# The decay and rate products of an RWKV-7 branch, taken in two passes of split operands; two staging buffers for raw weights

## The chip, the core and the metric

The kernel runs on one core of one Trainium2 chip. The metric is the time of one execution on the device, in microseconds (us); of a kernel that was run several times the median counts. One of the executions was recorded by the hardware profiler. Its page and its trace give the times of single instructions, of waits and of transfers. The engines go by the profile's names: PE is the matrix engine (PEld its weight loads), DVE the vector engine, ACT the scalar engine, POOL the GpSimd engine, and SP the engine whose queue issues all of this kernel's DMAs.

## What is computed

One layer over 2048 tokens of width 1024. The normalised input `h` is projected by one wide matrix into three branches and their gates: an RWKV-7 branch (8 heads of 64, with a delta-rule state), a sliding-window attention and a cross attention into 256 memory tokens. Each branch is gated and projected back, the three are merged by sigmoid gates, and a last projection is added to the input. All inputs and the output are float32.

The part that the change touches is the decay and the rate of the RWKV-7 branch, two products of low rank (64):

```
lw = token_shift_mix(p_w, mu_wa[0])
la = token_shift_mix(p_a, mu_wa[1])
w_log = -softplus(-(w0 + tanh(lw) @ w2)) - 0.5
decay = exp(-exp(w_log))
a = sigmoid(a0 + la @ a2)
```

`w2` and `a2` are 64 by 512. In the kernel they lie in one tile `w2a2`, `w2` in partitions 0 to 63 and `a2` in 64 to 127.

## The kernel before

**Blocks of tokens.** `build` runs four blocks of 512 tokens (the loop at L831). Tokens lie along the free axis, channels along the partitions. For each block: the low-rank inputs are projected and shifted (`proj` and `shift`, L832 and L833, then a tanh over the upper half of the partitions, L834); then two streams of work are woven together by given costs (`weave`, L865). `stream_r` holds the RWKV branch, four pairs of heads one after the other (`rwkv_pair`). `stream_f` holds everything else: in the first block the keys and values of the memory (`mem_kv`), then cross attention, window attention, merges and gates. After the streams come the merge of the RWKV branch, the norm of the next block's input (`x_norm`) and the output projection. What a function issues in between its `yield`s goes out in one piece. A scheduler then orders the instructions of each engine, which run strictly in that order.

**Products in three passes.** The big products split each float32 operand into a rounded part (type `F32R`) and the rest, and add three products (`gemm3`, L180 to L182): rounded by rounded, rounded weights by the rest of the activations, and the rest of the weights by rounded activations. A block of weights is 128 by 512 raw numbers and feeds 12 matmuls of 128x512, or 6 for the memory's values (L344 to L346).

**Weight staging.** `wblock` (L155) makes a block ready. In the first block of tokens it loads the raw weights into a tile `wraw` (L161, SP), ACT writes the rounded part into `whl` (L162), POOL subtracts to get the rest (L163), and the finished pair is stored to DRAM (`k`, L166, SP). The pool has three buffers for `wraw` and three for `whl`. The later blocks of tokens load the finished pair straight into `whl` (L158). The memory's weights are used once and not stored. On SP the store of a block stands directly ahead of the load that takes over the raw buffer of that block.

**The low-rank products.** In each pair, behind the projection of the keys (`proj` at L380 and `shift` at L381), there are two plain float32 matmuls with 64 rows each, L383 from the upper half of the partitions and L385 from the lower half. They write the PSUM tiles `pw` and `pa`, from a ring of two buffers (`rw_ps`). ACT takes a tanh of each (L387, L389). Then the rest of the previous pair is done (`rest`, L580 to L592). Its four transposes (L584) need a tile of the same ring, which comes free when L387 has read `pw`.

**Small rings.** `rt` is a ring of six work tiles of 128x512 (`tmp`), `ibc` one of two tiles of 1 KB per partition, used for the squares of the norms (L201) and by the triangular solve (L456 to L462, L476).

Of the kernel before, what the change touches and what calls it, by code (L numbers as in the profile page):

```python
# [9 lines left out]
F32 = mybir.dt.float32  # L10
F32R = mybir.dt.float32r
BF16 = mybir.dt.bfloat16
I32 = mybir.dt.int32
AF = mybir.ActivationFunctionType
ALU = mybir.AluOpType
# [4 lines left out]
TB = 512  # L20
NG = 12
NRT = 6
# [6 lines left out]
B_R, B_K, B_V, B_WA, B_ZA, B_Q, B_SK, B_SV, B_ZB, B_XQ, B_ZC, B_G = 0, 4, 8, 12, 13, 17, 21, 22, 23, 27, 31, 35  # L29
# [12 lines left out]
def build(tc, A, nsb=4):  # L42
    nc = tc.nc
    es = ExitStack()
    V, S, G, PE = nc.vector, nc.scalar, nc.gpsimd, nc.tensor

    def pool(name, bufs, **kw):
        return es.enter_context(tc.tile_pool(name=name, bufs=bufs, **kw))

    cp = pool("cp", 1)  # L50
    wp = pool("wp", 3)
    xp = pool("xp", 1)
    hp = pool("hp", 1)
    rp = pool("rp", 1)
# [12 lines left out]
    def rw_ps():  # L67
        return ps.tile([128, 512], F32, name="rw", bufs=2)
# [13 lines left out]
    def const(name, shape, src=None):  # L82
        t = cp.tile(shape, F32, name="c_" + name)
        nc.sync.dma_start(t, A[name] if src is None else src)
        return t
# [22 lines left out]
    w2a2 = const("w2a2", [128, 512])  # L108

    def pcol(name, i=0):  # L110
        o, w = PV[name]
        return pv[:, o + i:o + i + 1]
# [13 lines left out]
    def dcol(name, i=0):  # L126
        return dv[:, DV[name][0] + i:DV[name][0] + i + 1]
# [27 lines left out]
    def wblock(src, key=None):  # L155
        w = wp.tile([128, 2, 512], F32R, name="whl")
        if key in kept:
            nc.sync.dma_start(w.bitcast(F32), kept[key])  # L158
            return w[:, 0], w[:, 1]
        raw = wp.tile([128, 512], F32, name="wraw")  # L160
        nc.sync.dma_start(raw, src)  # L161
        S.activation(w[:, 0], raw, AF.Copy)  # L162
        G.tensor_tensor(w[:, 1], raw, w[:, 0].bitcast(F32), op=ALU.subtract)  # L163
        if key is not None and nsb > 1:
            kept[key] = dp.tile([128, 2, 512], F32, name=f"k{len(kept)}")
            nc.sync.dma_start(kept[key], w.bitcast(F32))  # L166
        return w[:, 0], w[:, 1]
# [50 lines left out]
    def proj(blk, hT, n=TB):  # L218
        o = mm_ps()
        gemm3(o[:, :n], [(w, (hT[0][:, k, :n], hT[1][:, k, :n])) for k, w in enumerate(wtiles(A["w_in"][blk], 8, ("in", blk)))])  # L220
        return o
# [142 lines left out]
    def shift(o, blk, mu, omu, sb, tag, bufs=1):  # L364
        t = rp.tile([128, TB], F32, name=tag, bufs=bufs)
        S.activation(t, o, AF.Copy, scale=omu)
        V.scalar_tensor_tensor(t[:, 1:], o[:, :TB - 1], mu, t[:, 1:], op0=ALU.mult, op1=ALU.add)
        V.scalar_tensor_tensor(t[:, 0:1], carry[sb % 2][:, blk:blk + 1], mu, t[:, 0:1], op0=ALU.mult, op1=ALU.add)
        V.tensor_copy(carry[1 - sb % 2][:, blk:blk + 1], o[:, TB - 1:TB])
        return t  # L370

    def tmp(tag="rt", bufs=NRT):
        return rp.tile([128, TB], F32, name=tag, bufs=bufs)

    EV, OD = slice(0, 64), slice(64, 128)
# [3 lines left out]
    def rwkv_pair(p, sb, hT, lwla, yas):  # L379
        kp = proj(B_K + p, hT)  # L380
        k = shift(kp, B_K + p, pcol("mu_k", p), dcol("omu_k", p), sb, "rk_")  # L381
        pw = rw_ps()
        PE.matmul(pw, w2a2[EV, p * 128:(p + 1) * 128], lwla[EV], start=True, stop=True)  # L383
        pa = rw_ps()
        PE.matmul(pa, w2a2[OD, p * 128:(p + 1) * 128], lwla[OD], start=True, stop=True)  # L385
        th = tmp()
        S.activation(th, pw, AF.Tanh, scale=0.5, bias=dcol("hw0", p))  # L387
        ta = tmp()
# [65 lines left out]
        for s in range(31):  # L454
            n = 31 - s
# [23 lines left out]
        for b in (0, 64):  # L479
            u, l = slice(b, b + 32), slice(b + 32, b + 64)  # L480
# [16 lines left out]
        for b in (0, 64):  # L497
            u, l = slice(b, b + 32), slice(b + 32, b + 64)
# [25 lines left out]
        for c in range(NC_):  # L524
            pw = rw_ps()[:, :C]
# [35 lines left out]
            for e, h, Q in HH:  # L561
                to = Sst[h, p] if c == NC_ - 1 else Z[h, e, c + 1]
# [222 lines left out]
    def merge(i, yh, yl, accs, hT, first=False, orange=range(8), gates=None):  # L785
        for o in orange:
            yield 3.718
            w = [t.rearrange("p (k c) -> p k c", k=4) for t in wblock(A["w_proj"][i, o], ("proj", i, o))]
            g = gates[o] if gates else gate(i, o, hT)
            pp = mm_ps()  # L790
            gemm3(pp, [((w[0][:, k], w[1][:, k]), (yh[k], yl[k])) for k in range(4)])
            if first:
                acc = mp.tile([128, TB], F32, name="mB")
                V.scalar_tensor_tensor(acc, g, 1.0, pp, op0=ALU.add, op1=ALU.mult)
                accs.append(acc)
            else:
                V.scalar_tensor_tensor(g, g, 1.0, pp, op0=ALU.add, op1=ALU.mult)  # L797
                V.tensor_tensor(accs[o], accs[o], g, op=ALU.add)
# [31 lines left out]
    hT = x_norm(0)  # L830
    for sb in range(nsb):  # L831
        wa = proj(B_WA, hT)  # L832
        lwla = shift(wa, B_WA, pcol("mu_wa"), dcol("omu_wa"), sb, "lwla")  # L833
        S.activation(lwla[EV], lwla[EV], AF.Tanh)  # L834
        yas = []
        ya, yb, yc_ = ([], []), ([], []), ([], [])
        accs = []

        def stream_r():
            for p in range(4):  # L840
                yield from rwkv_pair(p, sb, hT, lwla, yas)
            pend.pop()()
            yield 0.412

        def stream_f():
            if sb == 0:
                yield from mem_kv()
            for h in range(4):
                yield from cross_head(h, sb, hT, *yc_)
            rope_tables(sb)  # L850
            yield from swa_kv(sb, hT)
            yield 6.938
            for j in range(4):
                yield from weave(swa_pair(j, sb, hT, *yb), merge(2, *yc_, accs, hT, first=True, orange=(2 * j, 2 * j + 1)))
            yield from merge(1, *yb, accs, hT)
            for o in range(8):
                gates.append(gate(0, o, hT))
                yield 5.908

        gates = []  # L860
        def slower(g, f):
            for d in g:
                yield f * d

        for _ in weave(stream_r(), slower(stream_f(), 1.531)):  # L865
            pass
        for p in range(4):
            split_y(yas[p], *ya, "a", p, sb)
        for _ in merge(0, *ya, accs, hT, gates=gates):
            pass  # L870
        if sb + 1 < nsb:
            hT = x_norm(sb + 1)
        output(sb, accs)
# [3 lines left out]
def weave(*gens):  # L877

    live = [[0.0, i, g] for i, g in enumerate(gens)]
    now = 0.0  # L880
    while live:
        live.sort(key=lambda x: x[:2])
        e = live[0]
        try:
            d = next(e[2])
        except StopIteration:
            live.pop(0)
            continue
        e[0] += d
        t = min(x[0] for x in live)  # L890
        if t > now:
            yield t - now
            now = t
# [64 lines left out]
```

## Time and profile before

| What | Value |
|---|---|
| Median of three runs | 2585.37 us (2582.68 to 2591.96) |
| The profiled execution, its own time | 2582.91 us |
| Span of its instructions | 2581.1 us |
| Mean granted clock of PE | 0.983 |
| PE, DVE, ACT, POOL busy | 2462.6, 1516.6, 894.2, 426.9 us |
| DMA | 407.38 MB, 158 GB/s on average |

The median is 2.5 us above the profiled execution. Busy times are those of engines that run side by side, and do not add up to the span. A busy PE may be one whose clock was lowered; the profile gives the granted clock by stretches. In the timeline each row has start, duration, engine, source line, operation and tiles, and in brackets the idle time ahead of it and what ended that.

### The profile page before, as it was taken

Reading aid. Unit: us, or ns where it says so; the run is one execution under the profiler, and the core shown is the slowest. Engines: PE = TensorE matmul, PEld = TensorE weight load, DVE = VectorE, ACT = ScalarE, POOL = GpSimd, SP = SyncE. Lnnn points to the kernel's source line nnn. Section 1 sums busy time; section 2 is a strip of 40 time slices with the busy share of each in tenths; the row PEclk is TensorE's granted clock in tenths of the full one; section 3 lists DMA queues with packets and bytes.
Section 4 is the critical chain, followed back from the end, with each engine's and each line's share of the span. In section 5 each row is a group of like instructions: output and inputs, shape, how many; then the busy total and the mean of one; then the engine's idle time right before and its main releaser. Section 6 shows DMA issues by size and latency. Waiting matters only on the chain.

```text
span 2581.1 us, 39422 instructions
## 1 busy us (share of the span) xinstructions
PE 2462.6 (95%) x14496; PEld 1873.3 (73%) x14496; DVE 1516.6 (59%) x4788; ACT 894.2 (35%) x1957; POOL 426.9 (17%) x394
## 2 busy tenths in 40 slices
PE   6898989989999999999999999999999999999999
PEld 5666666667777777777677777777777777777777
DVE  6767884753427675745345686563653768574623
ACT  5344534444323333331322334341231334332120
POOL 3432423425421100010000110010000110010000
PEclk9798989999999999999999999999999999999999
DMA  5344544547873334434464243435466333434546
GB/s 172 116 142 139 175 157 147 196 171 274 282 265 107 123 111 139 131 128 166 156 232 158 93 150 115 135 112 171 139 212 218 102 126 117 141 127 132 172 136 230
DMA packets 132528, 407.38 MB, mean 158 GB/s; under 512 B 15344, under 2 KB 15728, under 8 KB 132336
## 3 DMA queue, kind: packets, MB, share of 16 engines
q1 hardware_dynamic: 132336, 404.86, 46.8%
q8 instruction: 115, 1.88, 0.3%
q14 instruction: 77, 0.63, 0.1%
HBM read 313.58 MB, written 91.23 MB: 157 GB/s over the span
## 4 chain that ended last, share of the span: by engine, by line
PE 56%; DVE 9%; DMA 4%; ACT 2%; issue 1%; POOL 0%; SPq 0%; ACTq 0%; DVEq 0%; POOLq 0%
PE mm L180 13%; PE mm L182 13%; PE mm L181 13%; DMA whl<-k 3%; DVE ibc L457 2%; PE rw L441 1%; DVE ibc L458 1%; DVE Yi L459 1%; PE oo L771 1%; PE rw L556 1%; PE rw L546 1%; PE rw L528 1%; PE mm L815 1%; PE mm L816 1%; PE mm L817 1%
## 5 line engine op out<-in xcount | busy, mean ns | idle before, releaser
L180 PE MATMUL mm<-hH,whl 128*128 128x512 f32 x1888 | 772.3, 409 | 15.9 <-DMA whl<-k 10.6
L182 PE MATMUL mm<-hH,whl 128*128 128x512 f32 x1888 | 764.9, 405 | 3.7 <-POOL whl L163 3.4
L181 PE MATMUL mm<-hL,whl 128*128 128x512 f32 x1888 | 762.1, 404 | 0.0
L180 PEld LDWEIGHTS mm<-hH,whl 128*128 128x128 f32 x1888 | 359.0, 190 | 102.2 <-issue 15.9
L182 PEld LDWEIGHTS mm<-hH,whl 128*128 128x128 f32 x1888 | 358.1, 190 | 80.8 <-POOL whl L163 6.8
L181 PEld LDWEIGHTS mm<-hL,whl 128*128 128x128 f32 x1888 | 359.4, 190 | 68.6 <-issue 0.2
L163 POOL TENSOR_TENSOR whl<-wraw,whl 128x512 fp32r<-128x512 f32 x174 | 229.5, 1324 | 387.3 <-ACT whl L162 363.9
L458 DVE TENSOR_TENSOR ibc<-ibc,Yi 128x248 f32<-128x248 f32 (+30 forms) x496 | 168.1, 339 | 8.9
L459 DVE TENSOR_TENSOR Yi<-Yi,ibc 128x248 f32<-128x248 f32 (+30 forms) x496 | 161.3, 325 | 0.5
L162 ACT ACTIVATE whl<-wraw 128x512 fp32r<-128x512 f32 x174 | 108.3, 628 | 143.6 <-PE mm L182 65.4
L542 ACT ACTIVATE SP<-Z,Pt 64x64 f32<-64x64 f32 x256 | 88.3, 345 | 195.8 <-DVE Z L563 192.4
L797 DVE SCALAR_TENSOR_TENSOR g<-g,mm 128x512 f32<-128x512 f32 x64 | 43.8, 684 | 186.1 <-PE mm L182 164.0
L457 DVE STREAM_SHUFFLE ibc<-Nc 128x248 f32<-128x248 f32 (+30 forms) x496 | 151.9, 310 | 0.0
L180 PE MATMUL mm<-yh,whl 128*128 128x512 f32 x384 | 150.8, 393 | 0.3
L181 PE MATMUL mm<-yl,whl 128*128 128x512 f32 x384 | 150.5, 392 | 0.0
L182 PE MATMUL mm<-yh,whl 128*128 128x512 f32 x384 | 150.2, 391 | 0.0
L782 ACT ACTIVATE g<-mm 128x512 f32<-128x512 f32 x96 | 57.3, 597 | 248.3 <-PE mm L182 248.0
L145 POOL TENSOR_SCALAR st<-st 128x4 f32<-128x4 f32 (+1 forms) x32 | 8.3, 259 | 646.0 <-DVE st L722 397.2
L751 ACT ACTIVATE g<-g,mxs,st 128x256 f32<-128x256 f32 (+1 forms) x128 | 74.4, 582 | 67.4 <-DVE mxs L744 67.3
L563 DVE SCALAR_TENSOR_TENSOR Z<-rw,Pt,SP 64x64 f32<-64x64 f32 x224 | 63.4, 283 | 53.2 <-PE rw L556 48.8
L539 DVE COPY W<-rw 128x64 f32<-128x64 f32 x128 | 28.7, 224 | 101.7 <-PE rw L528 100.5
L822 DVE SCALAR_TENSOR_TENSOR g<-mm,g 128x512 f32<-128x512 f32 x16 | 11.1, 692 | 126.5 <-PE mm L817 126.5
(1737 smaller groups left out, 4141.5 us busy)
## 6 DMA issues: line engine op xcount, KB each, us to landing
whl<-k SPq DMA_DIRECT2D x474, 512.0 KB, 3.3
k<-whl SPq DMA_DIRECT2D x158, 512.0 KB, 2.9
wraw<-in_w_in SPq DMA_DIRECT2D x118, 256.0 KB, 3.6
g<-in_x SPq DMA_DIRECT2D x36, 256.0 KB, 4.6
out<-g SPq DMA_DIRECT2D x32, 256.0 KB, 2.9
rt<-in_x SPq DMA_DIRECT2D x28, 256.0 KB, 4.1
wraw<-in_w_proj SPq DMA_DIRECT2D x24, 256.0 KB, 3.6
wraw<-in_w_out SPq DMA_DIRECT2D x16, 256.0 KB, 3.5
```

The lines of the kernel that those rows point to most:

```text
L162: S.activation(w[:, 0], raw, AF.Copy)
L163: G.tensor_tensor(w[:, 1], raw, w[:, 0].bitcast(F32), op=ALU.subtract)
L180: PE.matmul(out, lh, rh, start=i == 0, stop=False)
L181: PE.matmul(out, lh, rl, start=False, stop=False)
L182: PE.matmul(out, ll, rh, start=False, stop=i == n - 1)
L457: V.stream_shuffle(bc[:, :, :n], Nc[:, :, s + 1:], [s] * 32)
L458: V.tensor_tensor(bc[:, :, :n], bc[:, :, :n], Y[:, :, s:s + 1].to_broadcast([128, NC_, n]), op=ALU.mult)
L459: V.tensor_tensor(Y[:, :, s + 1:], Y[:, :, s + 1:], bc[:, :, :n], op=ALU.add)
L542: S.activation(SP[h], Z[h, e, c], AF.Copy, scale=Pt[h, c, C:C + 1])
L563: upd = V.scalar_tensor_tensor(to, pS[h], Pt[h, c, C:C + 1], SP[h], op0=ALU.mult, op1=ALU.add)
L751: S.activation(prs[b][:, i, m0:], prs[b][:, i, m0:], AF.Exp, scale=r2[:, b, i:i + 1], bias=mx[:, b, i:i + 1], accum_out=mx[:, b, 2 + i:3 + i])
L782: S.activation(t, gp, AF.Tanh, scale=0.5)
```

## The change

- `wraw` gets two buffers instead of three.
- The low-rank inputs (`lwla`) go into a tile of the ring `rt`. From it two tiles `lww` and `lwa` of type `F32R` are made once for each block of tokens. `lww` holds the rounded tanh(lw) in its upper 64 partitions and the rest of it in the lower 64. `lwa` holds the rounded la in the lower and its rest in the upper half. That is two copies on ACT and two subtractions on DVE.
- In each pair the 128 columns of `w2a2` are split as well: four copies on ACT write the rounded weights, each half of the partitions into both halves of the tile `wh`; two subtractions on POOL write the rest into `wl`. Both tiles come from the ring `ibc`.
- The two float32 matmuls become four `F32R` ones: two with 128 rows (rounded weights by the stacked activations, one for `pw`, one for `pa`) and two with 64 rows (rest of the weights by rounded activations).

```diff
-        raw = wp.tile([128, 512], F32, name="wraw")
+        raw = wp.tile([128, 512], F32, name="wraw", bufs=2)
...
-        pw = rw_ps()
-        PE.matmul(pw, w2a2[EV, p * 128:(p + 1) * 128], lwla[EV], start=True, stop=True)
-        pa = rw_ps()
-        PE.matmul(pa, w2a2[OD, p * 128:(p + 1) * 128], lwla[OD], start=True, stop=True)
+
+        wt = w2a2[:, p * 128:(p + 1) * 128]
+        wh = rp.tile([128, 2, 128], F32R, name="ibc", bufs=2)
+        wl = rp.tile([128, 2, 128], F32R, name="ibc", bufs=2)[:, 0]
+        for i, h in enumerate((EV, OD)):
+            for to in (EV, OD):
+                S.activation(wh[to, i], wt[h], AF.Copy)
+            G.tensor_tensor(wl[h], wt[h], wh[h, i].bitcast(F32), op=ALU.subtract)
+        pw, pa = rw_ps(), rw_ps()
+        for i, o in enumerate((pw, pa)):
+            PE.matmul(o, wh[:, i], lwla[i], start=True, stop=False)
+        for i, (o, h) in enumerate(((pw, EV), (pa, OD))):
+            PE.matmul(o, wl[h], lwla[i][h], start=False, stop=True)
...
-        lwla = shift(wa, B_WA, pcol("mu_wa"), dcol("omu_wa"), sb, "lwla")
+        lwla = shift(wa, B_WA, pcol("mu_wa"), dcol("omu_wa"), sb, "rt", NRT)
         S.activation(lwla[EV], lwla[EV], AF.Tanh)
+        lw = lwla
+        lwla = [rp.tile([128, TB], F32R, name="lw" + n) for n in "wa"]
+        for t, h, l in zip(lwla, (EV, OD), (OD, EV)):
+            S.activation(t[h], lw[h], AF.Copy)
+            V.tensor_tensor(t[l], lw[h], t[h].bitcast(F32), op=ALU.subtract)
```

## The prediction

> **What bounds the kernel now.** I read the page first: busy shares, then the granted clock, then the chain that ended last.
>
> ```profile
> span 2581.1 us, 39422 instructions
> ...
> PE 2462.6 (95%) x14496; PEld 1873.3 (73%) x14496; DVE 1516.6 (59%) x4788; ACT 894.2 (35%) x1957; POOL 426.9 (17%) x394
> ...
> PEclk9798989999999999999999999999999999999999
> ...
> PE 56%; DVE 9%; DMA 4%; ACT 2%; issue 1%; POOL 0%; SPq 0%; ACTq 0%; DVEq 0%; POOLq 0%
> ```
>
> PE is busy for 95% of the span, and the chain runs mostly over it. So an edit counts by what it does to PE: the slots it takes and the waits it ends or makes. The clock row is below full only early. Then the windows by stage (columns: length, then busy us of PE, PEld, DVE, ACT, POOL, then granted clock, DMA share, GB/s).
>
> ```profile
> 27.00:130.00 103.00, 80.20 (x463) 61.90 (x461) 76.97 (x206) 40.00 (x84) 43.00 (x41) 0.87 0.38 122
> ...
> 600.00:745.00 145.00, 140.11 (x620) 113.24 (x619) 45.20 (x64) 53.46 (x101) 67.67 (x55) 0.99 0.84 290
> ...
> 1356.00:1966.00 610.00, 599.44 (x3588) 457.86 (x3587) 356.62 (x1186) 195.79 (x438) 46.83 (x49) 1.00 0.44 148
> ```
>
> In a later block of tokens PE lacks some 10 us of 610. At the end of the first block (600 to 745) PE is as full, but there the DMA share is 0.84: this is the stage that stages raw weights through the buffers which the change cuts. In the memory stage (27 to 130) PE is idle for 23 us and has other things to wait for. Last, who makes PE wait in the three later blocks (columns: total us, times, longest).
>
> ```profile
> PE mm L180 <- DMA whl<-k: 10.6, 17, 2.7
> PE rw L584 <- ACT rt L387: 4.6, 6, 0.8
> ```
>
> The second row is the wait that the low-rank products cause: the transposes of the previous pair get their PSUM tile only after the tanh L387.
>
> **The change part by part. 1, the products on PE.** How two float32 products run shows in the timeline of one pair, and in the row of that line over the run.
>
> ```profile
> L383 PE MATMUL rw<-lwla,c_w2a x32: 589/641/693, 30.9 to 2358.0; 64*128 64x512 f32 x32
> ```
>
> ```profile
> 1008.85 0.39 PE L181 MATMUL mm<-hL,whl 128*128 128x512 f32 x1
> 1009.08 0.39 PE L182 MATMUL mm<-hH,whl 128*128 128x512 f32 x1
> 1009.40 0.69 PE L383 MATMUL rw<-lwla,c_w2a 64*128 64x512 f32 x1
> 1009.40 0.69 PE L385 MATMUL rw<-lwla,c_w2a 64*128 64x512 f32 x1
> 1009.93 0.59 PE L383 MATMUL rw<-lwla,c_w2a 64*128 64x512 f32 x1
> 1010.56 0.69 ACT L387 ACTIVATE rt<-rw,dv 128x512 f32<-128x512 f32 x1 [0.37 <-PE rw L385]
> 1011.30 0.66 PE L584 MATMUL rw<-c_ident,rt 128*128 128x128 f32 x4 [0.77 <-ACT rt L387]
> ```
>
> A rounded matmul takes a slot of 1009.08 - 1008.85 = 0.23 us. The 16 calls of L383 leave 32 records, two each, and L383 and L385 start together: the two products lie side by side on the two halves of the rows. From L182 to the transposes 1011.30 - 1009.08 = 2.22 us pass, of which 0.77 is the wait for L387.
>
> After: four rounded matmuls at the slot 0.23 (one with 64 rows costs the same, I take; its output is as wide). In the order of the changed kernel the next three matmuls of the value projection then stand ahead of the transposes, where they stood behind them. So up to the transposes only L182 and the four count as new: 5 x 0.23 = 1.15 us in place of 2.22, a gain of 1.07. Is the tile free by then? `pw` is whole 1009.08 + 3 x 0.23 + 0.39 after its last matmul starts, about 1010.2; a tanh of 0.69 ends at about 1010.9; the transposes stand eight slots after 1009.08, at 1010.92. Just in time. The order shows this in six pairs, the second and third of each later block: **-6.4**.
>
> In the first pair of a later block no transposes follow:
>
> ```profile
> 760.12 0.63 ACT L834 ACTIVATE lwla<-lwla 64x512 f32<-64x512 f32 x1 [1.00 <-DVE carry L369]
> ...
> 763.45 0.39 PE L182 MATMUL mm<-hH,whl 128*128 128x512 f32 x1
> 763.76 0.69 PE L383 MATMUL rw<-lwla,c_w2a 64*128 64x512 f32 x1
> 764.82 0.50 PE L180 MATMUL mm<-hH,whl 128*128 128x512 f32 x1
> 765.16 0.39 PE L181 MATMUL mm<-hL,whl 128*128 128x512 f32 x1
> ```
>
> From L182 to L181 it is 765.16 - 763.45 = 1.71 us, where two plain slots would be 0.46. So the products cost 1.25, after the change 4 x 0.23 = 0.92: -0.33, or up to -0.57 if the late L180 goes too. Four such pairs: **-1.8**. In the fourth pairs of the three later blocks the next matmul waits for its weights by DMA (the row of 10.6 us above), and two transposes still stand directly behind the products: -0.3 each, **-0.9**. Three pairs of the first block have the transposes at other places: between 0.33 and 1.07, I take 0.75, **-2.3**. Together **-11.4**; bounds -4 (only the bare products, 12 x 0.33) and -13 (all 12 pairs at 1.07).
>
> The Trainium skill, page "FP8 and Floating Point Precision", section "TensorE Precision Notes", says that true FP32 takes four passes through the array. Taken one after the other, that would make eight slots of the two products, 1.84 us, and the new four would save 16 x 0.92 = 14.7 us. The trace differs: two records for a product, the two products side by side, 1.12 us from 1009.40 to the end of the second records (1009.93 + 0.59), so the sum goes by the rows.
>
> **2, the added splits.** Nearest rows, for a 64-partition operation on each engine (columns: total, mean ns, idle before):
>
> ```profile
> L542 ACT ACTIVATE SP<-Z,Pt 64x64 f32<-64x64 f32 x256 | 88.3, 345 | 195.8 <-DVE Z L563 192.4
> ...
> L677 POOL COPY Vt<-Vt 128x128 f32<-128x128 f32 x3 | 1.3, 442 | 9.8 <-PE oo L771 9.8
> ...
> L717 DVE TENSOR_TENSOR g<-g,g 64x512 fp32r<-64x512 f32 x32 | 23.9, 746 | 2.9 <-ACT g L716 2.1
> ```
>
> ACT gets 64 small copies, 64 x 0.35 = 22 us, and eight of 64x512 at 0.63; POOL 32 at up to 0.44; DVE eight at 0.75. None is the bound (35%, 17%, 59% busy). In the order, the copies and subtractions of a pair stand well ahead of its products, at the start of the previous pair's scan; what they hold up there is the ACT copies of that scan, one to four of 0.35 us. I take +0.1 for each of 15 pairs, **+1.5** (0 to +4). The splits at a block's start: L834 ends at 760.75, the first product starts at 763.76, 3.0 us of cover, and two ACT copies at 0.63 with a subtraction of 0.75 add 2.0. **0**; without that cover up to 2.0 in each of four blocks. The wait at the first products of all, at 30.9 us, falls in the memory stage.
>
> **3, two raw buffers at the end of the first block.** Here a block of weights feeds 12 matmuls, 12 x 0.23 = 2.7 us of PE. What the staging takes:
>
> ```profile
> 648.09 1.28 POOL L163 TENSOR_TENSOR whl<-wraw,whl 128x512 fp32r<-128x512 f32 x1 [1.86 <-ACT whl L162]
> ...
> 649.39 0.33 SPq L166 DMA_DIRECT2D k<-whl  x1
> 649.77 0.42 SPq L161 DMA_DIRECT2D wraw<-in_w_in  x1
> 652.33 0.60 ACT L782 ACTIVATE g<-mm 128x512 f32<-128x512 f32 x1 [2.04 <-PE mm L182]
> 652.83 0.62 ACT L162 ACTIVATE whl<-wraw 128x512 fp32r<-128x512 f32 x1
> 653.52 1.28 POOL L163 TENSOR_TENSOR whl<-wraw,whl 128x512 fp32r<-128x512 f32 x1 [1.86 <-ACT whl L162]
> ...
> 657.77 0.60 ACT L782 ACTIVATE g<-mm 128x512 f32<-128x512 f32 x1 [2.04 <-PE mm L182]
> ```
>
> ```profile
> wraw<-in_w_in SPq DMA_DIRECT2D x118, 256.0 KB, 3.6
> g<-in_x SPq DMA_DIRECT2D x36, 256.0 KB, 4.6
> ```
>
> PE's pace: from 652.33 to 657.77 two blocks were used, 2.72 us for one. The way of one raw buffer round: subtraction starts (648.09), load issued behind the store (649.77, 1.68 later), landing 3.6 (the median of these loads), then ACT at once and the next subtraction 0.69 after it (653.52 - 652.83): 1.68 + 3.6 + 0.69 = 5.97 us. With three buffers that is 1.99 a block, well below 2.72. With two it is 2.99: **0.27 short for each block**.
>
> ```profile
> 591.00:640.00 49.00, 10.71 (x17) 0.97 0.83 281
> 640.00:700.00 60.00, 13.10 (x21) 1.00 0.86 289
> 700.00:745.00 45.00, 7.54 (x12) 1.00 0.85 303
> ```
>
> These are the instances of L162 by stretch (columns: length, ACT busy, clock, DMA share, GB/s). The first and last stretch have other work between, so of 50 blocks I count 38 as dense (the 17 and the 21): 38 x 0.27 = 10.3. The three finished pairs in `whl` are a cushion of about one block, 3.2 us by the same recursion, and POOL's other subtractions of 1.28 in this stage put some 2 back: **+9**. Bounds by the landing: a little over 3 us hides it all (5.44 - 2.37 = 3.07), 4.6, the other row, makes the way 6.97 and a block 0.77 short.
>
> **4, the memory stage.** Its blocks of values feed only six matmuls, so two buffers are late there too, by 2 to 7 us in the same recursion. But PE waits there in any case:
>
> ```profile
> PE rw L482 <- DVE ibc L462: 5.4, 1, 5.4
> ```
>
> This wait for the triangular solve takes up most of it: **+1** (0 to +6), and the changed order at the first block's start (the low-rank projection now goes ahead of the memory norm's transposes) is 0, give or take 4.
>
> **Sum** against the profiled execution's own 2582.9 us: -11.4 + 1.5 + 0 + 9 + 1 = +0.1, so 2583. The median shown is 2.5 above that execution: **2586** on the median.
>
> **The rivals.**
>
> *The staging costs more (slower).* One mechanism: the two raw buffers at 591 to 700. At a DMA share of 0.84 the loads may land as late as the row of 4.6 us. Then 38 x 0.77 = 29, less the cushion of 3.2, is +26 in place of +9, net +17: 2602. Point of decision: slower at all from a landing of 3.6, by over 0.5% from 4.4. Against: the 118 loads themselves have a median of 3.6, and two buffers put fewer loads in flight.
>
> *The gain does not come.* The splits stand late behind something on ACT or POOL, or the transposes still wait: the 11.4 fall away, +11.5, 2597. Against: ACT and POOL are far from full.
>
> *The staging is hidden.* If the landing is nearer 3.1 (fewer loads at once), the +9 is about 0 and the net -9: 2576; with all pairs at 1.07, 2574, and less the +1.5, 2573.
>
> *The clock.* The new pauses could lower the clock:
>
> ```profile
> 632.00:640.00 8.00, 6.20 (x21) 4.62 (x20) 0.00 (x0) 1.86 (x3) 6.71 (x7) 0.79 0.65 200
> ```
>
> ```profile
> 634.53 0.61 PE L182 MATMUL mm<-hH,whl 128*128 128x512 f32 x1 [1.80 <-POOL whl L163]
> ```
>
> After a pause of 1.80 us the next matmuls take 0.61, and these 8 us have a granted clock of 0.79: 0.21 x 8 = 1.7 us lost. Pauses of 0.27 a block are far shorter; only if they gather into four of such length does it cost 7 more: 2592. The Trainium skill, page "TensorE: Matmul & The Clock Gate", section "Part 1: The HAM clock gate (the "warmup" mystery)", says that the clock halves after at least one idle window of about 3.4 us; by that rule no pause here would be long enough. The row shows a slower clock after 1.80 us already.
>
> **How the numbers follow.** Chances: my forecast (2580 to 2594) 0.39; the staging costs more (2594 to 2609) 0.27; the staging is hidden (2571 to 2579) 0.20; the gain does not come 0.08; the clock 0.06. About 0.5% (13 us) is what a measurement of this kernel can tell from no change: under 2572.5 is faster, over 2598.3 slower. Slower: most of the costly staging (0.22), half of the lost gain (0.04), ends of the others (0.03): 0.29. Faster: the hidden staging at its best, 0.10. Within 0.5%: 0.61. The range takes in the forecast, the hidden staging from its upper end and the costly staging up to its bound of 26 less the gains: 2572 to 2606.
>
> **What would show it.** The products: from the last matmul of the keys to the transposes some 1.9 us with three more matmuls in it, and no wait of L593 for the tanh in the second and third pairs. The three later blocks shorter by 2 to 3 us each. The staging: PE waits for L162 or L163 between 600 and 700 that add to about 9 us, and the subtractions of POOL at 2.99 a block. The splits: no wait of the products for POOL or ACT. The forecast is wrong if the landing of the raw loads is away from 3.6 us, if the wait goes from L387 to another tile of the ring, or if the clock row falls.

## The result, and the profile after

The changed kernel is slower: 2613.48 us in the median of six runs (2603.24 to 2620.51), beside 2586.04 for the kernel before. The ratio is **1.0097, with a 95% interval of 1.0080 to 1.0115**, some 25 us (it goes by the means of the runs, 2612.2 and 2587.0; the medians are 27.4 apart). The forecast was 2586 with a range of 2572 to 2606, so the time lies outside it, on the side of the first rival. The profiled execution of the changed kernel took 2606.03 us, 23.1 more than the profiled one of before.

The head of its page, the row of the clock and the chain:

```profile
span 2604.2 us, 39593 instructions
...
PE 2482.0 (95%) x14496; PEld 1883.9 (72%) x14496; DVE 1511.3 (58%) x4796; ACT 918.8 (35%) x2029; POOL 443.1 (17%) x426
...
PEclk8898989999999999999999999999999999999999
...
PE 59%; DVE 6%; DMA 3%; ACT 1%; issue 1%; SPq 0%; POOL 0%; ACTq 0%; DVEq 0%
```

PE has as many matmuls recorded as before, and yet is busy 19.4 us longer; the time without PE grew by 3.7 us only. A busy PE that takes longer for the same work ran at a lower clock, or stalled between matmuls that overlap. To find the place, the span is cut where the same instruction stands in both traces: the tanh at each block's start (L834, now L843) and the first scan of each pair. The first block of tokens ends at 760.1 us before and at 788.1 after, **+28.0**; the three later blocks take 1821.1 before and 1816.2 after, **-4.9**. All of the loss is in the first block, the one that stages raw weights. Its last three stretches, before:

```profile
165.00:296.00 131.00, 118.69 (x716) 86.38 (x715) 102.45 (x286) 61.47 (x127) 47.90 (x41) 0.94 0.42 140
296.00:459.00 163.00, 150.73 (x892) 112.57 (x891) 110.15 (x340) 71.05 (x162) 54.74 (x43) 0.96 0.51 172
459.00:760.00 301.00, 278.82 (x1454) 215.50 (x1453) 138.24 (x333) 113.92 (x227) 122.46 (x98) 0.98 0.69 238
```

and the same three after:

```profile
158.00:293.00 135.00, 121.60 (x714) 88.40 (x713) 102.81 (x288) 62.34 (x130) 46.66 (x42) 0.91 0.39 135
293.00:465.00 172.00, 154.85 (x898) 114.25 (x897) 112.15 (x339) 73.83 (x168) 57.56 (x46) 0.93 0.47 163
465.00:788.00 323.00, 290.90 (x1445) 217.17 (x1442) 131.66 (x333) 114.37 (x229) 125.10 (x100) 0.96 0.66 225
```

About the same matmuls take 4, 9 and 22 us more. In each stretch the granted clock is 0.02 to 0.03 lower, and the last has 10 us more without PE (323.00 - 290.90 against 301.00 - 278.82). Who made PE wait, over the whole run, before and then after:

```profile
PE mm L180 <- ACT whl L162: 4.2, 1, 4.2
PE mm L182 <- POOL whl L163: 3.4, 3, 1.8
```

```profile
PE mm L180 <- ACT whl L162: 15.7, 9, 5.8
...
PE mm L182 <- POOL whl L163: 12.0, 19, 1.8
```

These are the two engines that make a block of weights ready: 7.6 us in 4 waits have become 27.7 in 28. Between 600 and 700 PE itself waits 5.7 us for them where it waited 1.8, less than the 9 that the prediction named as a sign; the weight loads (PEld) wait 12.6 where they waited 2.4.

The low-rank products themselves went nearly as forecast in this pair. The pair that was shown of before (at 1009), in the changed kernel:

```profile
1035.20 0.39 PE L182 MATMUL mm<-hH,whl 128*128 128x512 f32 x1
...
1035.42 0.39 PE L392 MATMUL rw<-lww,ibc 128*128 128x512 f32 x1
...
1035.65 0.39 PE L392 MATMUL rw<-lwa,ibc 128*128 128x512 f32 x1
...
1035.97 0.50 PE L394 MATMUL rw<-lww,ibc 64*128 64x512 f32 x1
...
1035.97 0.50 PE L394 MATMUL rw<-lwa,ibc 64*128 64x512 f32 x1
...
1036.40 0.50 PE L180 MATMUL mm<-hH,whl 128*128 128x512 f32 x1
1036.51 0.69 ACT L396 ACTIVATE rt<-rw,dv 128x512 f32<-128x512 f32 x1 [0.19 <-PE rw L394]
...
1037.25 0.66 PE L593 MATMUL rw<-c_ident,rt 128*128 128x128 f32 x4
```

From L182 to the next projection it is 1.20 us where 1.15 was worked out. The two products with 64 rows start together, as the float32 ones did. Three matmuls of the projection stand ahead of the transposes, which come 2.05 us after L182 and start about 0.05 behind the end of the tanh. Eight slots of 0.23, or 1.84, were forecast. This pair gained 0.86 us (the lag between the traces falls from 26.12 to 25.26 over it); 1.07 was forecast.

### The profile page after: what moved, and what is told of

Its sections match the earlier page's. It is cut to its first block, busy times and chain, and to the rows that moved or that the text cites. A ratio compares the mean times of both kernels' runs of the same rounds, so it can differ in the third digit from the quotient of the medians.

```text
span 2604.2 us, 39593 instructions
## 1 busy us (share of the span) xinstructions
PE 2482.0 (95%) x14496; PEld 1883.9 (72%) x14496; DVE 1511.3 (58%) x4796; ACT 918.8 (35%) x2029; POOL 443.1 (17%) x426
## 4 chain that ended last, share of the span: by engine, by line
PE 59%; DVE 6%; DMA 3%; ACT 1%; issue 1%; SPq 0%; POOL 0%; ACTq 0%; DVEq 0%
PE mm L180 14%; PE mm L182 14%; PE mm L181 13%; DMA whl<-k 3%; DVE ibc L466 1%; PE rw L450 1%; PE oo L780 1%; PE rw L565 1%; DVE ibc L467 1%; PE rw L555 1%; DVE Yi L468 1%; PE rw L537 1%; PE oo L669 1%; PE mm L825 1%; PE mm L826 1%; PE mm L824 1%
## 5 line engine op out<-in xcount | busy, mean ns | idle before, releaser
L182 PE MATMUL mm<-hH,whl 128*128 128x512 f32 x1888 | 770.6, 408 | 12.4 <-POOL whl L163 12.0
L182 PEld LDWEIGHTS mm<-hH,whl 128*128 128x128 f32 x1888 | 360.0, 191 | 99.2 <-POOL whl L163 24.9
L163 POOL TENSOR_TENSOR whl<-wraw,whl 128x512 fp32r<-128x512 f32 x174 | 229.3, 1323 | 398.2 <-ACT whl L162 376.5
L162 ACT ACTIVATE whl<-wraw 128x512 fp32r<-128x512 f32 x174 | 108.5, 630 | 178.8 <-DMA wraw<-in_w_in 71.3
L182 PE MATMUL mm<-yh,whl 128*128 128x512 f32 x384 | 150.4, 392 | 0.0
L791 ACT ACTIVATE g<-mm 128x512 f32<-128x512 f32 x96 | 57.1, 595 | 248.3 <-PE mm L182 248.0
L180 PEld LDWEIGHTS mm<-yh,whl 128*128 128x128 f32 x384 | 72.4, 188 | 18.8 <-issue 3.5
```

The source lines that it names most:

```text
L180: PE.matmul(out, lh, rh, start=i == 0, stop=False)
L182: PE.matmul(out, ll, rh, start=False, stop=i == n - 1)
L791: S.activation(t, gp, AF.Tanh, scale=0.5)
```

## The experiments

**Theory A:** the loss is the staging through two raw buffers, all over the first block and not at its end only. **Rival B:** the split itself, with its operations on ACT and POOL and the changed order, costs in the first block. Every ratio below is to the kernel before on the same chip, with its 95% interval; 0.001 is 2.6 us. "First" is the end of the first block and "later" the length of the three later ones, in us of the one profiled execution; the kernel before has 760.1 and 1821.1.

| Run | Raw buffers | Split products | Load ahead of store | Ratio | First | Later |
|---|---|---|---|---|---|---|
| changed kernel | 2 | all | no | 1.0097 (1.0080 to 1.0115) | 788.1 | 1816.2 |
| e1 | 2 | none | no | 1.0085 (1.0070 to 1.0100) | 779.9 | 1823.3 |
| e2 (ya 3) | 3 | all | no | 1.0016 (1.0005 to 1.0027) | 767.4 | 1820.0 |
| e3 (ring 11) | 3 | all | no | 1.0103 (1.0085 to 1.0120) | 768.8 | 1844.3 |
| e4 (DVE subtracts) | 2 | all | no | 1.0126 (1.0108 to 1.0145) | 802.0 | 1814.1 |
| e5 (ya 3) | 3 | none | no | 0.9999 (0.9985 to 1.0014) | 767.0 | 1825.1 |
| e6 (ya 3) | 4 | none | no | 0.9978 (0.9966 to 0.9991) | 758.7 | 1822.9 |
| e7 (ya 3) | 3 | later blocks | no | 0.9994 (0.9980 to 1.0008) | 761.8 | 1818.6 |
| e8 | 1 | none | no | 1.1680 (1.1649 to 1.1710) | 1196.2 | 1823.8 |
| e9 | 2 | later blocks | no | 1.0086 (1.0068 to 1.0104) | 789.9 | 1822.1 |
| e10 (ya 2) | 4 | later blocks | no | 1.0029 (1.0009 to 1.0048) | 758.1 | 1829.9 |
| e11 | 2 | all | yes | 0.9997 (0.9981 to 1.0012) | 768.1 | 1816.8 |
| e12 (ya 3) | 3 | all, splits on DVE | no | 1.0019 (1.0002 to 1.0037) | 771.4 | 1816.2 |
| e13 | 2 | none | yes | 0.9993 (0.9980 to 1.0005) | 765.8 | 1819.7 |
| e14 | 3 | none | yes | 0.9982 (0.9972 to 0.9993) | 760.4 | 1816.2 |
| e15 (ya 3) | 3 | all | yes | 1.0017 (1.0003 to 1.0031) | 769.6 | 1818.3 |
| e16 (ya 3) | 3 | later blocks | yes | 0.9986 (0.9975 to 0.9996) | 757.5 | 1816.5 |
| e17 (ya 3) | 3 | from second pair | yes | 0.9999 (0.9983 to 1.0015) | 760.8 | 1817.2 |
| e18 | 2 | from second pair | yes | 0.9977 (0.9965 to 0.9989) | 760.0 | 1818.2 |

e5, whose ratio is 0.9999, ends its first block 7 us later than before, so "first" alone, from one profile each, decides nothing below that.

### One half at a time: e1 to e3

e1 is the kernel before with this edit and no other:

```diff
-        raw = wp.tile([128, 512], F32, name="wraw")
+        raw = wp.tile([128, 512], F32, name="wraw", bufs=2)
```

> The kernel before with two raw buffers in place of three, and nothing else. Theory A (the staging with two raw buffers makes the whole loss, over all of the first block of tokens): slower than before by 27 to 33 us, since the changed kernel is 23 us slower in its profile and gains 4 to 5 us in the three later blocks; the first block ends some 27 us later, the later blocks take as long as before. Rival B (half of the loss, that of 200 to 580 us, comes from the split's own work and order in the woven part of the first block): only the end of the first block is late, 12 to 17 us slower.

Measured: 1.0085, 22 us slower. Both theories asked for another number (A for 27 to 33), but the buffers alone make most of the loss. Its last stretch, cut as above:

```profile
458.00:780.00 322.00, 292.08 (x1444) 218.45 (x1443) 130.50 (x333) 113.34 (x226) 125.40 (x97) 0.95 0.65 225
```

That is the row of the changed kernel over again. Set against before, the lag of e1 goes from -8.5 us at 200 (the two buffers even shorten the memory stage) to +5 at 600 and +19.9 at 760: 13 us are lost in the woven part, 15 at the end of the block, by these two profiles.

e2 is the changed kernel with three raw buffers; the 2 KB come from `ya`:

```diff
-        raw = wp.tile([128, 512], F32, name="wraw", bufs=2)
+        raw = wp.tile([128, 512], F32, name="wraw", bufs=3)
...
-            yt = yp.tile([128, TB], F32, name="ya")
+            yt = yp.tile([128, TB], F32, name="ya", bufs=3)
```

> The changed kernel with three raw buffers again; the room for the third comes from three instead of four buffers of the tile ya (results of the head pairs). Theory A: the loss of the first block goes, and the gain of the later blocks stays: 4 to 10 us faster than before. Rival B: the loss between 200 and 580 us stays, 8 to 14 us slower than before.

Measured: 1.0016. The loss goes, but no gain shows; the result lies between what the two theories gave. e3 takes the room from the stream tiles instead (`NG = 11`).

> As the run before it, but the room comes from the ring of the stream tiles, 11 instead of 12 buffers. If taking a buffer from ya or from this ring costs nothing, both give the same within 3 us; theory A again 4 to 10 us faster than the kernel before, rival B 8 to 14 us slower.

Measured: 1.0103. The taken buffer is dear: the later blocks are 23 us longer than before, while the first block ends as in e2. It says nothing more on the split.

### The subtraction on DVE: e4

```diff
-        G.tensor_tensor(w[:, 1], raw, w[:, 0].bitcast(F32), op=ALU.subtract)
+        V.tensor_tensor(w[:, 1], raw, w[:, 0].bitcast(F32), op=ALU.subtract)
```

> The changed kernel with two raw buffers, but the subtraction of a weight block runs on DVE (0.75 us by the row of a 64x512 subtraction, in place of 1.28 on POOL). If the way round of one raw buffer sets the pace at the end of the first block, it shrinks from 5.97 to about 5.4 us for two blocks, just PE's pace of 5.44, and the end of the first block (600 to 750 us) gains 8 to 14 us over the changed kernel. If the landing of the loads or the order on SP sets it, it gains under 3 us. In the woven part DVE is busier (58% of the span), which can cost some of it again.

Measured: 1.0126, slower still, by 7 us over the changed kernel; the first block ends at 802.0. A forecast of 8 to 14 us of gain over the changed kernel missed. The trace shows why it does not decide: at the end of the block both roundings L162 of a pair of blocks now stand on ACT directly behind the activation L791, which waits for PE (at 661.96 and 669.21, after 5.6 us of idle time each), and PE then waits 1.2 us for L162 (at 663.12 and 670.38). The order of ACT sets this pace, not the way round.

### Controls and doses: e5 to e8

e5 is the kernel before with `ya` in three buffers.

> The kernel before with three instead of four buffers of the tile ya, nothing else: the control for the run of the changed kernel with three raw buffers, which was 3 us (0.16%) slower than before. If the split itself costs in the first block what it gains later, ya with three buffers costs nothing here: within 2 us of the kernel before. If ya hid a gain of the split, this run is 3 to 8 us slower than before.

Measured: 0.9999. `ya` in three buffers costs nothing that shows, so the split of e2 really gained nothing net. e6 adds a fourth raw buffer to e5.

> The kernel before with four raw buffers (room from ya, three instead of four). If the way round of the raw buffers decides the first block, three are already enough at its end (5.97 us for three blocks is 1.99 a block, PE needs 2.72), so at most the waits for weight staging that are left before (about 9 us with the half-clock windows behind them) can go: 0 to 8 us faster than before. If the pace is set by something else, no change.

Measured: 0.9978, 6 us faster than the kernel before: even three raw buffers held it back a little. e7 is e2 with the products of the kernel before while `sb == 0`:

```diff
+        if sb == 0:
+            pw = rw_ps()
+            PE.matmul(pw, w2a2[EV, p * 128:(p + 1) * 128], lwla[EV], start=True, stop=True)
+            pa = rw_ps()
+            PE.matmul(pa, w2a2[OD, p * 128:(p + 1) * 128], lwla[OD], start=True, stop=True)
+        else:
...
```

> The changed kernel with three raw buffers (ya with three), and in the first block of tokens the plain float32 products of the kernel before; the split products only in the three later blocks. Theory: the split gains 3 to 5 us in the later blocks and costs in the first, where ACT and POOL stage weights as well: 1 to 6 us faster than before. Rival: the split gains nothing anywhere beyond the noise: within 1.5 us of the kernel before, or slower.

Measured: 0.9994 (0.9980 to 1.0008). The median is where the theory wanted it, but the interval holds no change at all, so the rival stands too. e8 has one raw buffer, `bufs=1`.

> The kernel before with one raw buffer. If the way round of a raw buffer (subtraction, store, load, landing, rounding: 5.97 us) sets the pace, the blocks at the end of the first block of tokens follow each other every 5.9 to 6.2 us, and the 174 raw blocks of the run take at least 174 x 5.97 = 1039 us, so that the first block ends at 1000 to 1080 us instead of 760: 240 to 320 us slower. If the loss with two buffers came from another cause, such as the order on SP, it grows by far less, under 100 us.

Measured: 434 us slower, more than the 240 to 320 expected; the first block ends at 1196 us. The subtractions of the weight blocks on POOL, the first and the last of five with all between them left out, and a window there:

```profile
903.13 1.27 POOL L163 TENSOR_TENSOR whl<-wraw,whl 128x512 fp32r<-128x512 f32 x1 [4.53 <-ACT whl L162]
...
930.65 1.28 POOL L163 TENSOR_TENSOR whl<-wraw,whl 128x512 fp32r<-128x512 f32 x1 [3.59 <-ACT whl L162]
```

```profile
800.00:1000.00 200.00, 128.29 (x399) 88.33 (x400) 21.24 (x29) 37.46 (x69) 51.53 (x43) 0.79 0.41 137
```

Four steps in 27.5 us are 6.9 us each: the way round of 6 us, lengthened by a slow load (issued at 910.48, in ACT at 915.78) and by POOL's other subtractions (L609, from 917.73 on). So the ring of raw buffers does set the pace. The loss is larger than the idle time of PE: PE is busy 2651.6 us, 189 more than before, and the granted clock is 0.79 in this window and 0.918 over the run.

### Which blocks of tokens: e9 and e10

e9 is e7 with two raw buffers and four of `ya`.

> The changed kernel (two raw buffers), with the plain float32 products in the first block of tokens and the split ones in the three later blocks. If the split costs 5 to 8 us in the first block and gains some 6 us in the later ones, this is 5 to 8 us faster than the changed kernel and 4 to 7 us faster than the kernel before with two raw buffers only (1.0085): a ratio of about 1.006 to the kernel before. If the split costs nothing in the first block, it equals the changed kernel (1.0097).

Measured: 1.0086. The second case (1.0097) lies in its interval, the first (1.006) does not: with two raw buffers taking the split out of the first block gained 3 us, give or take 6. Where PE waits for staging anyway, a delay of the split can hide in the wait; that was not shown. e10 is e7 with four raw buffers and two of `ya`.

> Four raw buffers, split products in the later blocks only; the room comes from ya, two buffers instead of four. Four raw buffers gave 0.9978 and the split in the later blocks gains about 6 us (0.9977 by itself): 8 to 12 us faster than before, ratio 0.9955 to 0.997, if two buffers of ya cost nothing. If ya with two costs, the end of each block of tokens is late.

Measured: 1.0029, slower. Its first block is short (758.1), but the later ones take 1829.9, 11 more than in e7, which has three buffers of `ya`: two buffers of `ya` cost there. A miss.

### The order on SP: e11, e13 and e14

e11 is the changed kernel with the store of a block put off until the load that takes over its raw buffer has been issued:

```diff
         nc.sync.dma_start(raw, src)
+        while len(stores) > 1:
+            nc.sync.dma_start(*stores.pop(0))
...
-            nc.sync.dma_start(kept[key], w.bitcast(F32))
+            stores.append((kept[key], w.bitcast(F32)))
```

> The changed kernel, but on SP the load that takes over a raw buffer stands ahead of the store of that block instead of behind it, so it is issued 0.38 us earlier. If the way round of the two raw buffers sets the pace at the end of the first block, it goes from about 6.2 to 5.8 us for two blocks, 0.19 us a block: over some 40 blocks 5 to 8 us faster than the changed kernel, ratio about 1.007. If transfers share a bandwidth, so that the order only swaps who waits, no difference from 1.0097.

Measured: 0.9997. **The whole loss is gone** (0.0100 of the ratio, 26 us), where 5 to 8 were expected. The medians of the transfers on the page, changed kernel and then e11 (KB each, us to landing), show what the expectation left out:

```profile
k<-whl SPq DMA_DIRECT2D x158, 512.0 KB, 2.9
wraw<-in_w_in SPq DMA_DIRECT2D x118, 256.0 KB, 3.6
```

```profile
k<-whl SPq DMA_DIRECT2D x158, 512.0 KB, 4.0
wraw<-in_w_in SPq DMA_DIRECT2D x118, 256.0 KB, 3.1
```

The load does not only start 0.38 us earlier, it also lands 0.5 us sooner, and the store 1.1 later: the one that is issued first lands sooner, as if the second waited for its bytes. The Trainium skill, page "DMA: Bandwidth & Descriptors", section "Queues, rings and completion order", says that each DMA engine takes up the descriptors of a ring in their order; these two pairs of rows agree. One way round in the changed kernel (POOL, SP and ACT by their rows):

```profile
660.94 1.29 POOL L163 TENSOR_TENSOR whl<-wraw,whl 128x512 fp32r<-128x512 f32 x1 [1.32 <-ACT whl L162]
...
662.26 0.33 SPq L166 DMA_DIRECT2D k<-whl  x1
...
662.64 0.42 SPq L161 DMA_DIRECT2D wraw<-in_w_in  x1
...
666.39 0.63 ACT L162 ACTIVATE whl<-wraw 128x512 fp32r<-128x512 f32 x1 [2.15 <-DMA wraw<-in_w_in]
...
667.11 1.29 POOL L163 TENSOR_TENSOR whl<-wraw,whl 128x512 fp32r<-128x512 f32 x1 [1.50 <-ACT whl L162]
```

and in e11:

```profile
651.57 1.29 POOL L168 TENSOR_TENSOR whl<-wraw,whl 128x512 fp32r<-128x512 f32 x1 [1.36 <-ACT whl L167]
...
652.89 0.33 SPq L164 DMA_DIRECT2D wraw<-in_w_in  x1
...
653.27 0.43 SPq L166 DMA_DIRECT2D k<-whl  x1
...
656.27 0.63 ACT L167 ACTIVATE whl<-wraw 128x512 fp32r<-128x512 f32 x1 [2.21 <-DMA wraw<-in_w_in]
...
656.98 1.29 POOL L168 TENSOR_TENSOR whl<-wraw,whl 128x512 fp32r<-128x512 f32 x1 [1.55 <-ACT whl L167]
```

6.17 us for two blocks have become 5.41, that is 3.09 and 2.71 for one; over ten such steps of the changed kernel (from 654.58) it is 3.17, over fourteen of e11 (from 640.62) 2.70. PE takes 2.72. The change sat just past the point where the ring is slower than PE, and this edit brings it back onto it.

e13 is e1 with this edit, without any split. Here and in the later runs a block also claims its buffer of `whl` only behind the load and the store, where e11 claims it first.

> The kernel before with two raw buffers and the load ahead of the store on SP, float32 products as before. If the store ahead of the load is the whole loss of the two buffers, the 22 us of the run with two raw buffers only (1.0085) go: ratio 0.998 to 1.003. Against it the changed kernel with the load first (0.9997) tells what the split is worth when staging does not bound the first block: if the split gains its 6 us of the later blocks net, this run is 4 to 8 us slower than that one (ratio 1.0015 to 1.003); if it costs in the first block what it gains later, they are equal.

Measured: 0.9993. The buffers' whole 22 us go here too, so the loss of two buffers is the load behind the store (e11 shows it without the later claim of `whl`). Against e11 (0.9997) the split is worth nothing net: 0.0004 slower, give or take 0.0020. e14 is the kernel before, three buffers, with that edit.

> The kernel before (three raw buffers) with the load ahead of the store on SP. Three buffers are enough at the end of the first block already (1.99 us a block against 2.72), so only the left waits for staging in the woven part and the half-clock windows behind them can go: 0 to 8 us faster, as with four raw buffers (0.9978). If the later stores come in the way of PE's buffers, slower.

Measured: 0.9982, 5 us faster, about as much as a fourth buffer (e6).

### Where the split loses what it gains: e12, e15 to e18

e12 is e2 with the splits of the low-rank weights on DVE:

```diff
-                S.activation(wh[to, i], wt[h], AF.Copy)
-            G.tensor_tensor(wl[h], wt[h], wh[h, i].bitcast(F32), op=ALU.subtract)
+                V.tensor_copy(wh[to, i], wt[h])
+            V.tensor_tensor(wl[h], wt[h], wh[h, i].bitcast(F32), op=ALU.subtract)
```

> The changed kernel with three raw buffers (ya with three; 1.0016), but the splits of the low-rank weights, four copies and two subtractions a pair, run on DVE instead of ACT and POOL. If the split costs in the first block because these six operations stand among the weight staging on ACT and POOL, this run is 3 to 7 us faster than that one (ratio about 0.9995). If DVE is the tighter engine in the woven part, or the cost is the changed order of PE, it is the same or slower.

Measured: 1.0019, the same as e2. Queueing among the weight staging on ACT and POOL is not what costs, unless the same work cost as much on DVE, which no run takes apart. e15 is e2, and e16 is e7, with the load ahead of the store.

> The changed kernel with three raw buffers (ya with three, 1.0016) and the load ahead of the store. If staging was what the split paid for in the first block, it is 5 to 9 us faster than the kernel before (ratio 0.9965 to 0.998). If the split costs PE or the clock something in the first block whatever the staging does, ratio 1.000 to 1.002.

> As the run before it, with the float32 products in the first block of tokens and the split ones later. If the split costs in the first block by itself, this is the fastest of the four, 6 to 12 us faster than the kernel before (ratio 0.9955 to 0.9975); if not, it equals the run before it within 3 us.

Measured: 1.0017 and 0.9986. So with three raw buffers the split costs in the first block even with the load ahead of the store: 0.0031 with an uncertainty of 0.0018, 8 us. (With the store first, e2 against e7, it is 0.0022 with 0.0018.) e17 is e15 with float32 products in the very first pair, and the low-rank inputs of the first block split only behind them; e18 is the same with two raw buffers and four of `ya`.

```diff
+        if sb == 0 and p == 0:
...
+            lwla[:] = split_lw(lwla[0])
+        else:
```

> The changed kernel with three raw buffers and the load first (1.0017), but the first pair of the first block of tokens keeps the float32 products, and the low-rank inputs of that block are split only behind them. If the split loses its 8 us of the first block at the start, where it stands ahead of the memory norm's transposes, they go: 4 to 9 us faster than that run, ratio 0.9985 or lower, as with the split in the later blocks only (0.9986). If the loss lies in the pairs two to four, ratio 1.001 to 1.002 as before.

> The same with two raw buffers and four of ya, the buffers of the changed kernel. With the load first two buffers cost nothing (0.9993 without the split), so by the first theory of the run before it 0.997 to 0.9990, by the second 1.000, like the changed kernel with the load first (0.9997).

Measured: 0.9999 against 1.0017, and 0.9977 against 0.9997 (e11). Each step alone is inside its uncertainty; together they are 0.0019 with 0.0014, 5 us, and in the profiles the first block ends 8.8 and 8.1 us earlier. So the medians put the greater part of the 8 us at the start of the first block, though both numbers are uncertain by some 4 us, and e18 also differs from e11 in the claim of `whl`. What is late there stands in the traces: the norm of the memory, whose squares use the ring `ibc` of two buffers that the split's `wh` and `wl` now take first. The first and last of its four squares and its first transposes on PE, in e15:

```profile
33.02 0.63 ACT L207 ACTIVATE ibc<-g 128x512 bf16<-128x512 f32 x1 [0.22 <-PE rw L398]
...
37.13 0.61 ACT L207 ACTIVATE ibc<-g 128x512 bf16<-128x512 f32 x1
```

```profile
41.14 0.41 PE L217 MATMUL rw<-c_ident,g 128*128 128x128 f32 x2 [2.10 <-ACT SP L557]
```

and in e17, its last square and its first transposes:

```profile
25.78 0.61 ACT L207 ACTIVATE ibc<-g 128x512 bf16<-128x512 f32 x1
```

```profile
36.12 1.12 PE L217 MATMUL rw<-c_ident,g 128*128 128x128 f32 x4 [1.93 <-ACT rt L416]
```

In e15 the first square waits for the split product L398, which reads `wh`. In all seven traces with the split in the first pair the last square starts between 37.0 and 43.6 us and the transposes at 41 or later; in the thirteen without it, by 31.0 and between 33 and 38. That this lateness makes the whole loss was not shown: no run gives the split a ring of its own.

e18 has the change's own buffers and beats both kernels: 6 us faster than before, 31 faster than the changed kernel. e6, e14 and e16 are level with it.

## Why the prediction was wrong, point by point

**Step 3, two raw buffers at the end of the first block (+9): the step that failed, in its size.** The mechanism was right: one way round of a raw buffer against PE's pace. e8 and e11 show it from both sides. The price is 22 us (e1). Three things were off.
- *The pace.* The way round was too short in its landing, which stood in the sum at 3.6 us, the median over the run. In the changed kernel the twelve loads that are issued from 654.32 to 688.01 reach ACT 3.9 us after their issue on average, with ACT idle and waiting for them; the slowest takes 5.0. POOL does nothing else between 654 and 690, and its subtractions from 654.58 to 686.32 come every 3.17 us on average, where 2.99 was forecast. With 2.72 for PE the shortage is 0.45, not 0.27, for each block. The end of the block lost 15 us in e1 where 9 were worked out.
- *The place.* Only 38 blocks of weights from 591 us on were counted. In the woven part ahead of it e1 lost 13 us by the profiles, and between 130 and 600 PE's waits for L162 and L163 are 16.1 us in 14 (before 5.8 in 3). The prediction priced that part at nothing without naming what hides it.
- *The clock.* The timed runs of before have a median clock of 0.980, those of the changed kernel 0.9765. Lost clock is (1 - 0.9765) x 2613 = 61 us against (1 - 0.980) x 2586 = 52: some 10 of the 27 us between the medians, if PE had work all that time. It falls in the woven part; at the end of the block, from 591 to 770, the clock stays at 1.00. So it is in part the same time as the 13 us of the place, and is not to be added to it.

The slowest of the twelve loads, on SP and then on ACT:

```profile
666.01 0.42 SPq L161 DMA_DIRECT2D wraw<-in_w_in  x1
```

```profile
671.04 0.63 ACT L162 ACTIVATE whl<-wraw 128x512 fp32r<-128x512 f32 x1 [3.52 <-DMA wraw<-in_w_in]
```

The measured terms come to the measured loss: 22 us for the buffers, some 8 for the split in the first block and some 5 gained in the later ones make 25. That is an estimate, as the 8 were measured with three raw buffers.

**Step 1, the products (-11.4).** The way in which they gain was right, the sizes were too high. Over the single pairs of the later blocks, the lag between the two traces falls by 0.85 us in each second and third pair (1.07 worked out) and by 0.18 in each first pair (0.33 worked out). In the fourth pairs it rises, by 0.31, 0.35 and 0.18, where -0.3 was worked out: the two transposes behind the products now wait for the tanh, a wait that the prediction took away in the other pairs and did not count here.

```profile
1164.39 0.44 PE L593 MATMUL rw<-c_ident,rt 128*128 128x128 f32 x2 [0.78 <-ACT rt L396]
```

The twelve pairs together make -4.8, the -4.9 between the profiles. Steps 1 and 2 gave 8.7 of gain less 1.2 of delay, that is -7.5. Eleven profiles with the split have 1817.6 us on average for the later blocks, six without it 1821.4 (e3, e8 and e10 left out, whose rings differ): **-3.8, give or take 2.9**. And in the first block, where step 1 put -2.7, the split costs some 8 (e15 against e16).

**Step 2, the splits hidden (+1.5).** In the later blocks right: no wait of the products for POOL or ACT appears, and e12 moved them without effect. At the start of the first block wrong: what step 4 put at "0, give or take 4" for the changed order there is a loss of 5 us by the medians and 8 by the profiles (e17, e18). The sum has no term for the ring `ibc`, which the split shares with the squares of the memory's norm.

**Step 4, the memory stage (+1).** The other way about: e1 stands 8.5 us ahead of before by 200 us. By this profile the two buffers cost nothing there. It was not asked why.

**The rivals.** "The staging costs more" came nearest (2602), in direction, and its cause was the one in part: the median landing of the run stayed at 3.6, but in the dense stretch the loads reached ACT after 3.9, not 4.6. Fewer loads at once did not bring the landing to 3.1, as "the staging is hidden" had it. "The clock" was given 0.06 and a rule that short pauses are harmless; it was part of what happened. "The gain does not come" was true in sum, and not for the reason named. The three sat on the same side, and were priced as if only one could come.

## What to carry to other kernels

A ring of staging buffers is priced by its whole way round against the consumer's pace, wherever the consumer is dense and not in the busiest stage only; close to balance, a few tenths of a microsecond on each block are the whole effect, so the landing is to be read in that stretch and not as a median of the run. Before a buffer is bought or sold, look at what stands ahead of its refill in the DMA queue: a load that is urgent belongs ahead of a store that is not, and here that was worth as much as the buffer. Waits of PE are to be counted with the clock that they cost behind them.

## What the runs showed of the hardware

**Behind a short pause the clock can be halved for 3.4 us.** In all traces the granted clock changes between 1.0 and 0.5 and stays there for multiples of 3.41 us. In e1, in a later block of tokens, after a pause of under 1 us among small matmuls, the waiting row and the windows around:

```profile
922.93 0.33 PE L238 MATMUL as__8421<-c_ident,rep 128*128 128x128 f32 x1 [0.86 <-DVE rep L237]
```

```profile
920.00:924.40 4.40, 3.53 (x21) 2.29 (x22) 3.38 (x7) 0.60 (x1) 1.26 (x1) 1.00 0.54 205
924.40:927.80 3.40, 3.40 (x17) 2.70 (x14) 3.33 (x7) 0.60 (x1) 0.00 (x0) 0.50 0.00 0
927.80:931.20 3.40, 3.40 (x19) 2.61 (x18) 3.31 (x6) 2.49 (x4) 0.00 (x0) 1.00 0.00 0
```

PE is never idle in the middle window, and runs at half speed: 1.7 us lost. In e1 this wait is followed by half speed in all three later blocks, before (0.87 us) and in the changed kernel (0.68) the same wait in two of three, so more than its length decides; where in the fixed grid of windows it falls is a likely reason, not a shown one. Among dense large matmuls pauses of 0.4 to 1.6 us left the clock at 1.00 (the changed kernel, 646 to 720). The rule of the Trainium skill that was weighed in the prediction (page "TensorE: Matmul & The Clock Gate", section "Part 1: The HAM clock gate (the "warmup" mystery)"), an idle window of about 3.4 us, has the length of the window as these traces show it, and not the pause that it takes. Between the profiles shown, before has 25 such windows, the changed kernel 34 and e1 37; but e5 and e11, which take the same time as before, have 31 and 32, so the count of one profile says little.

**Of two transfers of one queue, the one issued first lands sooner.** Swapping a store of 512 KB and a load of 256 KB that are issued 0.4 us apart took 0.5 us of landing from the load and put 1.1 us onto the store (medians of the run).

**Rounded products of 64 rows run side by side, and save next to nothing.** On separate halves of the rows they start together (both at 1035.97), but the next matmul follows 0.43 us later, where two slots of 0.23 are 0.46.
